# Seven products for eight in u and v, and the S5 projection placed after v, in a hybrid decoder block

## The chip, the cores and the metric

The kernel runs on one core of one Trainium2 chip. The metric is the time of one execution on the device in microseconds, the median of three runs. The engines are TensorE (PE: matrix products into banks of PSUM; weights are loaded by PEld beside it), VectorE (DVE), ScalarE (ACT), GpSimd (POOL) and SyncE (SP), which here only issues transfers. Each engine works through its own list of instructions in order: an instruction that waits holds up all that stands behind it on that engine, and nothing else.

## The reference

One layer for 1024 tokens of 1024 channels in float32. Only the first sub-layer is touched; cross-attention and the SwiGLU FFN follow it unchanged.

```python
h = rms_norm(x, g_mix_pre)
z = h @ w_in                        # columns: u 1024 | v 1024 | S5 512 | gate A 1024 | gate B 1024
u, v = split(gelu(z_gm))
v = layer_norm(v, ln_g, ln_b)       # over the 1024 channels of a token
sv = einsum('gts,bnsgc->bntgc', tril(w_s), v) + b_s   # 8 groups of 128 channels, chunks of 128 tokens
y_gm = u * sv
y = gelu(s5_scan(z_s5))             # 32 groups of 16 channels, 64 complex states each
y_s5 = y * sigmoid(y @ w_glu)
merged = sigmoid(z_ga) * (y_gm @ w_br_gm) + sigmoid(z_gb) * (y_s5 @ w_br_s5)
x = x + rms_norm(merged @ w_mix_out, g_mix_post)
```

## The kernel before

A float32 product is made of three products in the format fp32r: each operand is split into a high half and the rest, and `mm3` adds hi·hi, hi·lo and lo·hi. One matmul takes 128 channels and gives 128 by 512 results, so that a block of `n` steps over the contracted channels costs 3n matmuls. To split a tile is a cast on ACT (`put`, L525, for data; `split`, L102, for weights) and a subtraction on DVE (L526, L103), which reads what the cast wrote.

All engines follow an order that the program writes out by hand. The main line is the products; between groups of them `sub()` lets each background generator (`bg`) take a step, and where a step lands there its instructions stand in every engine's list. Weights come as a stream: `make_plan` lists them in the order of use, `load` (SP queue, three raw buffers `wr`) and `split` work up to three ahead. Tiles of data are 38 slots `act` of 128 by 1024; PSUM has 8 banks `ps`.

The stages of the first sub-layer (`go`, L1559): keys and values of the memory with x's norm beside them; `s5_in`; `gates` (both gates to DRAM, with the S5 scan, `s5_gen`, beside them); then

- `s5_out` (L805): the first two blocks of u, then `drain()`, which runs the background to its end: GELU of the four tiles of the scan's output y (L744), 32 transposes of it (L754), and their splits. Then y @ w_glu with its sigmoid, and the product with w_br_s5 (`bs`), scaled by gate B, to DRAM;
- `v_phase` (L859): v, tokens on the partitions, two halves of 512 columns, each for two halves of the tokens in four banks each. GELU reads the bank and sums along the row (L899). After the second column half `ln` runs beside what follows: four squares with sums (L873), a reciprocal root in some dozen tiny operations, and per tile of 128 tokens one operation on 128x1024 (scale by `ln_g`) and eight on 128x128 (`ln_b`, written by groups, `vg`);
- `gm_phase` (L920): u's blocks 2 to 7; beside blocks 4 to 7 the gates, 8 groups of two halves: four products of 128x128 with the turned triangle, bias, times u, split;
- `merge` (L956): both branches to `merged`.

Line numbers below are of before; the changed kernel has the same helpers some lines later (L515 is L519 there, L133 L134, L136 L140, L102 and L103 L103 and L104, L525 and L526 L529 and L530).

Of the kernel before, what the change touches and what calls it, by code (L numbers as in the profile page):

```python
# [36 lines left out]
class Builder:  # L37
    def __init__(self, ctx, tc, ins):
# [13 lines left out]
        self.live = 0  # L52
        self.raws, self.pairs = {}, {}

# [11 lines left out]
    def sub(self):  # L66
        """called between groups of products"""
# [15 lines left out]
    def pump(self, n=1):  # L83
        while n and self.nsp < len(self.plan) and self.live < NWS - 1 and self.nsp < self.cur + LOOK:
            self.split()
            n -= 1

    def load(self):
        while self.nd < len(self.plan) and self.nd < self.nsp + NRAW:
# [34 lines left out]
    def rsqrt_ops(self, y, v, t):  # L124
        """y = 1 / sqrt(v): a first guess from the bits, three steps of Newton"""
# [6 lines left out]
    def tt(self, out, a, b, op):  # L132
        self.nc.vector.tensor_tensor(out=out, in0=a, in1=b, op=op)  # L133

# [13 lines left out]
    def vexp(self, o, x, k, r, i):  # L148
        """o = exp(x); k, r: room; i: int32 room"""
# [58 lines left out]
    def s5_params_a(self):  # L208
# [25 lines left out]
        # powers of a = mag (cs, sn), pq: P | Q for d = 0..8  # L234
# [19 lines left out]
        # co = (a - 1) / lam  # L254
# [20 lines left out]
        # mag^8  # L275
# [14 lines left out]
    def s5_params_b(self):  # L290
        """tables of e^{i 8 theta c}: 16 entries low, 8 entries high; and a^{7-k}"""
# [45 lines left out]
    def s5_params_c(self):  # L337
        """b and c with the states on the partitions"""
# [49 lines left out]
    def s5_a(self, b):  # L388
        """a^{7-k} B and C a^d"""
# [26 lines left out]
    def s5_b(self, b):  # L416
        """U, the B side turned, and what a chunk's tokens give within it"""
# [34 lines left out]
    def s5_c(self, b):  # L452
        """the phases, the chunks' parts, the scan over chunks"""
# [40 lines left out]
    def s5_d(self, b):  # L494
        """the chunks' outputs"""
# [21 lines left out]
    def mm3(self, ps, a, b, first, last, more=False):  # L517
        """float32's product: a = hi + lo, b = hi + lo, each part exact in float32r"""
# [4 lines left out]
    def put(self, dst, src):  # L523
        """dst = (hi, lo) of what lies in src"""
# [10 lines left out]
    def tblock(self, ps, w, c, xs, n=8, every=2):  # L535
        """ps[128 columns of w, tokens]"""
# [5 lines left out]
    def nblock(self, pss, w, k0, xs, last):  # L542
        """pss[t][tokens, 512 columns of w]"""
# [34 lines left out]
    def turn(self, xs, gi, dst, ks=range(8)):  # L578
        """transposes of four row tiles, scaled by the gain, split"""
# [1043 lines left out]
```

## Time and profile before

| | before |
|---|---|
| median of three runs | 1670.44 us (1669.47, 1670.44, 1670.87) |
| span of the profiled execution | 1668.2 us |
| the profiled execution's own time | not recorded apart from its span; the median lies 2.2 us above the span |
| PE busy | 1639.3 us, 98% |
| DVE, ACT, POOL busy | 1130.1, 637.3, 5.9 us |
| u0 and u1's end, drain, `glu`, `bs` | 366.19 to 445.50 us |
| v's products | 445.50 to 532.54 us |
| u2 to u7 with the gates | 532.54 to about 620 us |

A row of the timeline gives the start, the duration and the work, with a count where equal instructions are merged; the bracket tells how long the engine had been idle and whom it waited for. The page's chain follows the work that ended last back from the end: the engine that holds most of it sets the time. A window gives the busy time of every engine in a stretch, and the clock that TensorE was granted there (1.00 is its higher level of 2.4 GHz).

### The profile page before, as it was taken

To read this page: it belongs to the slowest core of one execution; us is meant where nothing else is said; L and a number is where in the kernel's file an instruction comes from. 1 tells how busy PE (TensorE), PEld (TensorE's weight loads), DVE (VectorE), ACT (ScalarE), POOL (GpSimd) and SP (SyncE) were. 2 spreads that over 40 slices of the span, in tenths; PEclk is the share of its full clock that TensorE was granted. 3 is DMA by queue.
4 is the path that set the end of the run, shared out by engine and by line. 5 is a ranking of instruction groups with operands and counts; after the bars stand their busy time and mean duration, and the time that the engine had idled before them with its cause. 6 is when DMAs were issued, how large, how long until landed. Compare 5 with 4: busy or idle time off the path is not lost.

```text
span 1668.2 us, 20774 instructions
## 1 busy us (share of the span) xinstructions
PE 1639.3 (98%) x7856; PEld 1374.1 (82%) x7856; DVE 1130.1 (68%) x2049; ACT 637.3 (38%) x1104; POOL 5.9 (0%) x13
## 2 busy tenths in 40 slices
PE   6999999999999999999999999999999999999998
PEld 6898878887888888888888888888888888888886
DVE  5679779867214665447854577686778777666778
ACT  6632212234124232235553447753233223244454
POOL 0000000000000000000000000000000000000000
PEclk9999999999999999999999999999999999999999
DMA  8622222213511225434523153674544446363634
GB/s 278 196 59 92 68 71 93 88 50 113 203 51 54 60 81 171 151 140 146 170 76 115 63 186 117 207 243 131 187 141 165 157 153 206 129 237 130 218 112 171
DMA packets 198772, 228.58 MB, mean 137 GB/s; under 512 B 13296, under 2 KB 137232, under 8 KB 198672
## 3 DMA queue, kind: packets, MB, share of 16 engines
q1 hardware_dynamic: 173328, 171.27, 31.9%
q10 hardware_dynamic: 24768, 53.88, 8.7%
q0 software_dynamic: 576, 2.10, 0.3%
q8 instruction: 62, 1.02, 0.2%
q14 instruction: 38, 0.31, 0.1%
HBM read 169.15 MB, written 56.36 MB: 135 GB/s over the span
## 4 chain that ended last, share of the span: by engine, by line
PE 89%; DVE 6%; ACT 2%; issue 1%; DMA 1%; ACTq 1%; SPq 0%; DVEq 0%
PE ps L515 85%; DVE act L133 2%; PE ps L583 1%; DVE ws L103 1%; DVE act L526 1%; ACTq L449 1%; ACT jk L571 0%; PE ps L1132 0%; ACT ws L102 0%; PE ps L1086 0%; DVE act L136 0%; ACT act L525 0%; PE ps L504 0%; DVE act L140 0%; PE ps L474 0%
## 5 line engine op out<-in xcount | busy, mean ns | idle before, releaser
L515 PE MATMUL ps<-act,ws 128*128 128x512 f32 (+1 forms) x4248 | 973.3, 387 | 3.8 <-DVE act L526 2.5
L515 PEld LDWEIGHTS ps<-act,ws 128*128 128x128 f32 x4248 | 780.4, 188 | 162.3 <-DVE act L526 4.7
L515 PE MATMUL ps<-ws,act 128*128 128x512 f32 x1440 | 342.8, 395 | 0.0
L515 PEld LDWEIGHTS ps<-ws,act 128*128 128x128 f32 x1440 | 279.4, 207 | 46.9
L133 DVE TENSOR_TENSOR act<-act 128x512 f32<-128x512 f32 (+6 forms) x513 | 281.8, 578 | 7.1 <-ACT act L1418 0.5
L103 DVE TENSOR_TENSOR ws<-wr,ws 128x1024 fp32r<-128x1024 f32 x114 | 139.2, 1222 | 126.9 <-ACT ws L102 124.6
L515 PE MATMUL ps<-ws 128*128 128x512 f32 x852 | 193.3, 389 | 0.0
L515 PEld LDWEIGHTS ps<-ws 128*128 128x128 f32 x852 | 159.9, 188 | 33.2
L133 DVE TENSOR_TENSOR act<-ps,act 128x512 f32<-128x512 f32 x178 | 120.9, 684 | 60.5 <-PE ps L515 55.6
L102 ACT CAST ws<-wr 128x1024 fp32r<-128x1024 f32 x114 | 119.5, 1048 | 104.9 <-PE ps L515 69.5
L1211 ACT CAST ws<-tm 128x512 fp32r<-128x512 f32 x88 | 54.8, 622 | 168.3 <-PE ps L515 113.3
L133 DVE TENSOR_TENSOR ws<-act,ws 128x512 fp32r<-128x512 f32 x93 | 64.2, 690 | 67.4 <-ACT ws L1418 51.8
L133 DVE TENSOR_TENSOR ws<-tm,ws 128x512 fp32r<-128x512 f32 x88 | 60.8, 691 | 59.5 <-ACT ws L1211 58.5
L525 ACT CAST act<-act 128x512 fp32r<-128x512 f32 (+1 forms) x72 | 46.1, 643 | 114.4 <-DVE act L133 114.0
L133 DVE TENSOR_TENSOR ws<-wr,ws 128x512 fp32r<-128x512 f32 x115 | 78.7, 685 | 15.2 <-ACT ws L1211 15.2
L515 PE MATMUL ps<-act 128*128 128x256 f32 (+2 forms) x488 | 83.3, 318 | 0.0
L526 DVE TENSOR_TENSOR act<-act 128x512 fp32r<-128x512 f32 (+1 forms) x72 | 51.8, 720 | 42.5 <-ACT act L525 42.5
L515 PEld LDWEIGHTS ps<-act 128*128 128x128 f32 x488 | 72.3, 189 | 8.3
L1418 ACT CAST ws<-act 128x512 fp32r<-128x512 f32 x71 | 44.2, 622 | 89.5 <-PE ps L515 48.3
L526 DVE TENSOR_TENSOR act<-ps,act 128x512 fp32r<-128x512 f32 x56 | 40.8, 748 | 47.7 <-ACT act L525 47.7
L136 DVE SCALAR_TENSOR_TENSOR act<-act,st 128x128 f32<-128x128 f32 (+2 forms) x100 | 58.7, 639 | 0.6
L525 ACT CAST act<-ps 128x512 fp32r<-128x512 f32 x56 | 35.6, 668 | 45.3 <-PE ps L515 38.0
(133 smaller groups left out, 902.4 us busy)
## 6 DMA issues: line engine op xcount, KB each, us to landing
wr<-in_ffn_w_gu_dram SPq DMA_DIRECT2D x39, 512.0 KB, 4.6
actd<-act ACTq DMA_DIRECT2D x77, 256.0 KB, 2.1
wr<-actd SPq DMA_DIRECT2D x38, 512.0 KB, 3.7
wr<-in_w_in_dram SPq DMA_DIRECT2D x36, 512.0 KB, 3.6
act<-in_ffn_w_gu_dram SPq DMA_DIRECT2D x22, 512.0 KB, 4.8
act<-in_ffn_w_down_dram SPq DMA_DIRECT2D x44, 256.0 KB, 4.4
pd<-act ACTq DMA_DIRECT2D x17, 512.0 KB, 4.2
act<-pd SPq DMA_DIRECT2D x34, 256.0 KB, 3.6
```

Of the source, the lines that this page charges most:

```text
L102: self.nc.scalar.copy(hi, t)
L103: self.nc.vector.tensor_tensor(out=lo, in0=t, in1=hi.bitcast(F), op=ALU.subtract)
L133: self.nc.vector.tensor_tensor(out=out, in0=a, in1=b, op=op)
L136: self.nc.vector.scalar_tensor_tensor(out=out, in0=a, scalar=s, in1=b, op0=op0, op1=op1)
L449: nc.scalar.dma_start(tv[16 * k:16 * k + 16, :, 16 * k:128], kv[:, :, 0:128 - 16 * k])
L515: self.nc.tensor.matmul(ps, a, b, start=start, stop=stop, skip_group_check=more)
L525: self.nc.scalar.copy(dst[0], src)
L526: self.nc.vector.tensor_tensor(out=dst[1], in0=src, in1=dst[0].bitcast(F), op=ALU.subtract)
L583: self.nc.tensor.transpose(ps[:, t * 128:t * 128 + 128], x[:, k * 128:k * 128 + 128], self.ident)
L1211: self.nc.scalar.copy(t[:, 0:512], now)
L1418: nc.scalar.copy(w[:, h[0]], src)
```

## The change

Blocks 2 to 7 of u are taken in pairs (2,3), (4,5), (6,7): the products of two blocks by two halves of the contracted channels and two halves of the tokens, which are eight products of halves, become seven by Winograd's form of Strassen's scheme. v is taken in the same form, by halves of channels, columns and tokens, in eight banks: X and Y, four each. The seven are named 11, 21, T1, T2, 22, T3, T4 after the side of h that they take. The sums of h (`h_sums`: 24 operations) are formed on GpSimd during the S5 scan, spilled to DRAM and taken back and split (`h_split`) when the scan is over; the sums of weights (`uv_sides`: 28 operations on 128x512) are formed on GpSimd one product ahead, and split (`w_ops`). What a product gives beside its bank is added on DVE from PSUM.

The order becomes u0, u1, u's pairs, v, then `s5_out` with the gates (`gm_gen`) beside it. u is spilled to DRAM and taken back by the gates. The scan's output y is spilled after its GELU; `y_turn` takes it back and transposes it beside v's last product. `ln` uses two operations on 128x1024 per tile, and loads `ln_g` and `ln_b` itself; `ln(1)` (the second half of the tokens) starts beside v's product 21, `ln(0)` after T4.

```diff
     def go(self, out):
...
         self.gates()
+        self.bg(self.w_ops(self.uv_sides()), 1)
+        for m in range(2):
+            self.u_block(m)
+        self.plain = True
+        self.u_pairs()
+        self.v_phase()
         self.s5_out()
-        self.v_phase()
-        self.gm_phase()
         self.merge()
...
+    def h_sums(self):
...
+        for k in range(4):
+            a, b = self.slot(), self.slot()
+            for t, kk in ((a, k), (b, k + 4)):
+                hi, lo = self.hT[kk]
+                self.gt(t, hi.bitcast(F), lo.bitcast(F), A)
+                yield 2
+            (a0, a1), (b0, b1) = ((t[:, 0:512], t[:, 512:1024]) for t in (a, b))
+            self.gt(a0, a1, a0, S)
+            self.gt(a1, b1, a1, S)
+            nc.gpsimd.dma_start(self.td[2 * k], a)
...
+            self.gt(b1, b1, a0, S)
+            self.gt(b0, b0, b1, S)
+            nc.gpsimd.dma_start(self.td[2 * k + 1], b)
...
         for q in range(4):
-            y = self.yq.pop(q)
-            self.yT.append(self.pair())
-            for jh in range(2):
+            self.nc.scalar.dma_start(self.yd[q], self.yq.pop(q))
+        y = None
+        yield from self.h_split()
...
     def s5_out(self):
         nc = self.nc
-        for m in range(2):
-            self.u_block(m)
-        self.drain()
+        while len(self.yT) < 4 or not self.yok:
+            self.sub()
...
+    def y_turn(self):
+        ys = []
+        for q in range(4):
+            ys.append(self.slot())
+            self.nc.sync.dma_start(ys[q], self.yd[q])
+        yield 2
+        for q in range(4):
+            self.yT.append(self.pair())
+            for jh in range(2):
+                ps = self.bank()
+                for j in range(4):
+                    o = (4 * jh + j) * 128
+                    self.nc.tensor.transpose(ps[:, j * 128:j * 128 + 128], ys[q][:, o:o + 128], self.ident)
...
+                self.put(dst, ps.rearrange("p (j c) -> p j c", j=4))
+                yield 1
...
-            self.rms(st, 4)
-            if not vg:
-                vg.extend(self.slot() for _ in range(8))
+            yield from self.rms_slow(st, 4)
+            if half:
+                self.lng = self.bcast(i["gm_ln_g"][0]), self.bcast(i["gm_ln_b"][0])
+            lg, lb = self.lng
             for t in range(4):
-                yield 2
+                yield 1
                 v = vt[4 * half + t]
                 self.stt(v, v, st[:, 40 + t:41 + t], lg, ALU.add, ALU.mult)
-                for g in range(8):
-                    o = slice(g * 128, g * 128 + 128)
-                    n = 4 * half + t
-                    self.stt(vg[g][:, n * 128:n * 128 + 128], v[:, o], st[:, 16 + t:17 + t], lb[:, o], ALU.mult, ALU.add)
+                self.stt(v, v, st[:, 16 + t:17 + t], lb, ALU.mult, ALU.add)
...
+        run(X, "T3", False)
+        del self.fxs["T3"]
+        for t in range(4):
+            v = vt[4 + t]
+            self.tt(v[:, h1], X[t], v[:, h1], ALU.add)
+            gelu(v[:, h1], v[:, h1], st(1, 1, t))
+        v = None
+        self.bg(ln(1))
+        run(Y, "21", True)
...
+        for t in range(4):
+            self.tt(vt[t][:, h0], Y[t], vt[t][:, h0], ALU.add)
+            gelu(vt[t][:, h0], vt[t][:, h0], st(0, 0, t))
+        Y = None
+        self.bg(self.y_turn(), 1)
+        run(X, "T4", False)
...
+        for t in range(4):
+            gelu(vt[t][:, h1], X[t], st(0, 1, t))
+        X = None
+        self.bg(ln(0))
```

On PE, before, from the end of the scan: the last 18 products of u1 (L515), the 32 transposes of y (L754), `glu` and `bs` (288), and v (384).

```order
L515 MATMUL ps<-act,ws 128x512 x18
L754 MATMUL ps<-ident,act 128x128 x32
L515 MATMUL ps<-act,ws 128x512 x288
L515 MATMUL ps<-ws,act 128x512 x384
```

On PE, after, the same stretch: u1's rest and u's pairs (270), v up to the middle of T4 (306), then the transposes of y (L1071) between T4's products, `glu`, the triangles (L1176) and the first gate's four 128x128 products.

```order
L519 MATMUL ps<-act,ws 128x512 x270
L519 MATMUL ps<-ws,act 128x512 x306
L1071 MATMUL ps<-ident,act 128x128 x4
L519 MATMUL ps<-ws,act 128x512 x6
L1071 MATMUL ps<-ident,act 128x128 x4
L519 MATMUL ps<-ws,act 128x512 x6
L1071 MATMUL ps<-ident,act 128x128 x4
```

On PE, after, from T4's last six products on: the last three transposed groups, `glu`'s first 36 products, the triangles and the first gate.

```order
L519 MATMUL ps<-ws,act 128x512 x6
L1071 MATMUL ps<-ident,act 128x128 x12
L519 MATMUL ps<-act,ws 128x512 x36
L1176 MATMUL ps<-ident,act 128x128 x4
L519 MATMUL ps<-act,ws 128x512 x6
L1176 MATMUL ps<-ident,act 128x128 x4
L519 MATMUL ps<-act,ws 128x512 x6
L519 MATMUL ps<-act 128x128 x4
```

The transposes stood as one block ahead of `glu`; now they stand in T4, which still holds four banks, and the gates stand in `glu` and `bs`, the first 48 products after the last transposes.

On DVE, after, from the statistics of `ln(1)` to the subtractions of y's splits: L104 splits weights, L140 on 128x1024 is `ln`, L134 `act<-ps,act` empties product 21's banks, L530 splits y.

```order
L104 TENSOR_TENSOR ws<-wr,ws 128x1024
L140 SCALAR_TENSOR_TENSOR st<-st 128x4 x2
L134 TENSOR_TENSOR st<-st 128x4
L140 SCALAR_TENSOR_TENSOR st<-st 128x4 x2
L134 TENSOR_TENSOR st<-st 128x4
L140 SCALAR_TENSOR_TENSOR st<-st 128x4
L140 SCALAR_TENSOR_TENSOR act<-act,st 128x1024 x2
L134 TENSOR_TENSOR act<-ps,act 128x512 x4
L140 SCALAR_TENSOR_TENSOR act<-act,st 128x1024 x2
L104 TENSOR_TENSOR ws<-wr,ws 128x1024
L140 SCALAR_TENSOR_TENSOR act<-act,st 128x1024 x4
L530 TENSOR_TENSOR act<-ps,act 128x4x128 x3
L104 TENSOR_TENSOR ws<-wr,ws 128x1024
L530 TENSOR_TENSOR act<-ps,act 128x4x128 x4
```

Before, the eight subtractions of y (L526) had only weights' splits beside them, and `ln` stood behind v; now eight `ln` operations, four emptyings and two weights' splits stand in one row ahead of y's first subtraction.

On DVE, after, from the end of the statistics of `ln(0)` to the second pair of its four tiles: L134 with `tm` and L530 `act<-act` are `glu`'s product with the sigmoid and its split, L140 on 128x1024 is `ln(0)`, which the first gate's products read.

```order
L140 SCALAR_TENSOR_TENSOR st<-st 128x4 x2
L134 TENSOR_TENSOR st<-st 128x4
L140 SCALAR_TENSOR_TENSOR st<-st 128x4
L134 TENSOR_TENSOR tm<-act 128x512
L134 TENSOR_TENSOR act<-act,tm 128x512
L530 TENSOR_TENSOR act<-act 128x512
L140 SCALAR_TENSOR_TENSOR act<-act,st 128x1024 x4
L134 TENSOR_TENSOR tm<-act 128x512
L134 TENSOR_TENSOR act<-act,tm 128x512
L530 TENSOR_TENSOR act<-act 128x512
L140 SCALAR_TENSOR_TENSOR act<-act,st 128x1024 x4
```

Before, `ln`'s operations had u's blocks 2 and 3 beside them; now all eight of `ln(0)` and three groups of `glu` come ahead of the first gate's last product.

On SP, after, from the last weights of v (L924): `glu`'s and `bs`'s weights (L94), then `ln_g` and `ln_b`, then y (L1063).

```order
L924 DMA act<-in_w_in_dram 128x1024 x5
L94 DMA wr<-in_s_w_glu_dram 128x4x256 x2
L94 DMA wr<-in_w_br_s_dram 128x4x256 x2
L579 DMA act<-in_gm_ln_g_dram 128x1024
L579 DMA act<-in_gm_ln_b_dram 128x1024
L1063 DMA act<-yd 128x1024 x4
L94 DMA wr<-in_w_br_s_dram 128x4x256 x2
```

On SP, before, `ln_g` and `ln_b` (L575) stood ahead of v's last weights:

```order
L835 DMA act<-gbd 128x1024 x2
L93 DMA wr<-in_w_in_dram 128x2x512
L575 DMA act<-in_gm_ln_g_dram 128x1024
L575 DMA act<-in_gm_ln_b_dram 128x1024
L93 DMA wr<-in_w_in_dram 128x2x512 x2
L93 DMA wr<-in_w_in_dram 128x8x128 x6
```

They now stand behind a load into the raw buffer that the first of `glu`'s weights has to leave, and ahead of y.

## Rows read from the trace of the kernel before

**Rows 1.** The page: busy time of TensorE, and the last chain by engine.

```profile
PE 1639.3 (98%) x7856; PEld 1374.1 (82%) x7856; DVE 1130.1 (68%) x2049; ACT 637.3 (38%) x1104; POOL 5.9 (0%) x13
...
PE 89%; DVE 6%; ACT 2%; issue 1%; DMA 1%; ACTq 1%; SPq 0%; DVEq 0%
```

**Rows 2.** Timeline, PE, 366 to 446 us: start, duration, work [idle before, releaser].

```profile
366.19 4.34 PE L515 MATMUL ps<-act,ws 128*128 128x512 f32 x18
370.38 3.65 PE L754 MATMUL ps<-ident,act 128*128 128x128 f32 x32
373.79 0.48 PE L515 MATMUL ps<-act,ws 128*128 128x512 f32 x1
...
380.85 64.81 PE L515 MATMUL ps<-act,ws 128*128 128x512 f32 x278 [0.36 <-DVE act L526]
```

**Rows 3.** Windows: busy per engine (instructions), TensorE's granted clock, DMA share, GB/s.

```profile
80.00:120.00 40.00, 40.00 (x209) 38.88 (x210) 30.15 (x160) 10.40 (x27) 0.00 (x0) 1.00 0.25 65
120.00:180.00 60.00, 60.00 (x286) 50.22 (x286) 55.12 (x174) 16.47 (x34) 0.00 (x0) 1.00 0.28 91
370.00:385.00 15.00, 12.69 (x57) 9.03 (x56) 11.66 (x13) 12.41 (x14) 0.00 (x0) 0.77 0.11 36
```

**Rows 4.** Timeline, PE, 440 to 540 us: v's products.

```profile
445.50 87.20 PE L515 MATMUL ps<-ws,act 128*128 128x512 f32 x384
```

**Rows 5.** Timeline, PE, 614 to 622 us: the last gate before the merge.

```profile
618.70 0.50 PE L515 MATMUL ps<-act,ws 128*128 128x512 f32 x1 [0.54 <-ACT act L525]
```

**Rows 6.** Timeline, POOL, whole span: its select on the triangles.

```profile
543.29 1.09 POOL L906 TENSOR_SCALAR_AFFINE_SELECT act<-act 128x1024 f32<-128x1024 f32 x1 [470.25 <-DVE st L142]
```

**Rows 7.** Timeline, DVE, 508 to 548 us: small operations beside it.

```profile
543.41 0.99 DVE L133 TENSOR_TENSOR st<-st 128x4 f32<-128x4 f32 x1
```

**Rows 8.** Lines by form, ACT, 366 to 620 us: count | busy, mean ns | idle before.

```profile
L744 ACT ACTIVATE act<-act 128x1024 f32<-128x1024 f32 x4 | 3.9, 1052 | 0.0
L525 ACT CAST act<-act 128x512 fp32r<-128x512 f32 x23 | 14.3, 620 | 47.0 <-DVE act L133 47.0
L525 ACT CAST act<-ps 128x512 fp32r<-128x512 f32 x8 | 7.9, 1154 | 0.2 <-PE ps L754 0.2
L899 ACT ACTIVATE act<-ps 128x512 f32<-128x512 f32 x16 | 9.6, 599 | 39.4 <-PE ps L515 39.4
L873 ACT ACTIVATE jk<-act,st 128x1024 bf16<-128x1024 f32 x8 | 9.2, 1149 | 4.1 <-DVE st L140 4.0
L873 ACT ACTIVATION_READ_ACCUMULATOR jk<-act,st 128x1 f32 x8 | 1.5, 187 | 0.0
L102 ACT CAST ws<-wr 128x1024 fp32r<-128x1024 f32 x20 | 21.0, 1050 | 57.9 <-PE ps L515 36.9 <-DVE act L133 11.1 <-DMA mbd<-act 9.9
L821 ACT ACT_TABLE_LOAD x1 | 1.3, 1283 | 0.0
```

**Rows 9.** Timeline, ACT, 402 to 446 us: the issue of one transfer.

```profile
409.40 0.36 ACTq L852 DMA_DIRECT2D mbd<-act  x1
```

**Rows 10.** Lines by form, DVE, 366 to 700 us.

```profile
L103 DVE TENSOR_TENSOR ws<-wr,ws 128x1024 fp32r<-128x1024 f32 x28 | 34.3, 1224 | 45.8 <-ACT ws L102 45.8
L526 DVE TENSOR_TENSOR act<-act 128x512 fp32r<-128x512 f32 x39 | 27.0, 692 | 26.9 <-ACT act L525 26.9
L133 DVE TENSOR_TENSOR act<-ps,act 128x512 f32<-128x512 f32 x31 | 21.3, 691 | 46.5 <-PE ps L515 46.5
L136 DVE SCALAR_TENSOR_TENSOR act<-act,st 128x1024 f32<-128x1024 f32 x8 | 10.2, 1278 | 0.0
L526 DVE TENSOR_TENSOR act<-ps,act 128x512 fp32r<-128x512 f32 x8 | 8.4, 1116 | 8.0 <-ACT act L525 8.0
L136 DVE SCALAR_TENSOR_TENSOR st<-st 128x4 f32<-128x4 f32 x12 | 2.0, 163 | 0.4
```

**Rows 11.** DMA issues: size, median us from issue to landing.

```profile
act<-gbd SPq DMA_DIRECT2D x8, 512.0 KB, 6.0
act<-in_gm_ln_g_dram SPq DMA_DIRECT2D x1, 512.0 KB, 6.1
```

More of the change, by code (lines that the diff above doesn't have):

```diff
@@ L694, in xgen @@
             self.bg(self.s5_gen(), 5)
+            self.bg(self.h_sums(), 2)
         self.bg(xgen())
@@ L758, in s5_in, with hx @@
+    def hx(self, name, k):
+        while name not in self.sides:
+            self.sub()
+        if name in ("11", "T1", "21", "22"):
+            o = 0 if name in ("11", "21") else 512
+            return tuple(x[:, o:o + 512] for x in self.hT[k + (4 if name[0] == "2" else 0)])
+        return self.fx(name, k)
     def s5_in(self):
@@ L803, in u_block, with later, w_ops @@
                 self.rel()
+        self.later(self.ud[m], u)
+    def later(self, *new):
+        while self.late:
+            self.nc.scalar.dma_start(*self.late.pop(0))
+        if new:
+            self.late.append(new)
+    def w_ops(self, gen):
+        while self.nsp < self.bar:
+            yield 1
+        now = None
+        while True:
+            t = None
+            if now is not None:
+                while self.live >= NWS:
+                    yield 1
+                t = self.ws.tile([P, 1024], R, name="ws", tag="ws")
+                self.live += 1
+                self.nc.scalar.copy(t[:, 0:512], now)
+            nxt = next(gen, ())
+            if nxt:
+                for x in nxt[1]:
+                    self.gt(*x)
+            if t is not None:
+                self.tt(t[:, 512:1024], now, t[:, 0:512].bitcast(F), ALU.subtract)
+                self.ops.append(t)
+            if nxt == ():
+                self.bar = len(self.plan)
+                return
+            now = nxt[0]
+            yield 1
@@ new lines, in ln, with run @@
+            if not half:
+                lg = lb = self.lng = None
+                self.vok = True
+        X, Y = ([self.bank() for _ in range(4)] for _ in range(2))
+        def run(ps, name, first):
+            for k in range(4):
+                x = self.hx(name, k)
+                w = self.take()
+                for t in range(4):
+                    c = slice(t * 128, t * 128 + 128)
+                    self.mm3(ps[t], tuple(z[:, c] for z in x), (w[:, h0], w[:, h1]), first and k == 0, k == 3, not first)
+                    if t % 2:
+                        self.sub()
+                self.live -= 1
+                x = w = None
@@ new lines, in v_phase @@
+        st = lambda half, cb, t: sums[half][:, 32 + cb * 4 + t:33 + cb * 4 + t]
+        gelu = lambda o, x, acc: nc.scalar.activation(out=o, in_=x, func=AF.Gelu_apprx_tanh, accum_out=acc)
+        run(X, "11", True)
+        for t in range(4):
+            vt[t] = self.slot()
+            nc.scalar.copy(vt[t][:, h0], X[t])
+        run(Y, "T1", True)
+        for k in range(4):
+            self.hT[k] = None
+        for t in range(4):
+            vt[4 + t] = self.slot()
+            nc.scalar.copy(vt[4 + t][:, h1], Y[t])
```

245 lines of the change are left out of this document (189 added, 56 removed).

## The prediction

> **What bounds the kernel now.** I read the page first, then PE's timeline over the stages that the change touches, then windows over the S5 scan, then the groups by line of ACT and DVE, for durations. PE is busy for 98% of the span and carries 89% of the chain that ended last [rows 1]: the kernel is bound by TensorE's products, so products that go away are worth their time, and anything that keeps PE waiting is paid in full. Between the scan's end at 366.19 and the merge, PE waits in two places only. One is y's turn: its 32 transposes start at 370.38, the products that need y's splits begin at 373.79, and ten of them last until 380.85 [rows 2], 7.06 us in place of 2.27 at the 0.227 us per product that v shows (87.20 us for 384 [rows 4]). In that window the granted clock is 0.77 [rows 3], a mean over stretches at 1.2 and 2.4 GHz. The other is the last gate, 0.54 us [rows 5].
>
> **What goes.** Each pair of u's blocks takes 84 products for 96, three times: 36 fewer. v takes 336 for 384: 48 fewer. 84 x 0.227 = 19.1 us. The stall at y's turn, 7.06 - 2.27 = 4.8 us, and the slower products behind it, 64.81 us for 278 where 63.0 are due [rows 2], 1.8 us: 6.6 in all. The last gate's 0.5: the gates now end inside `bs`. Sum of gains: **26.2 us**. They are gains only if what replaces those stalls is hidden.
>
> **What comes, beside the S5 scan.** `h_sums` are 8 operations of 128x1024 and 16 of 128x512 on GpSimd. The trace has no such sum; the nearest row is the select on 128x1024, 1.09 us [rows 6], which gives 8 x 1.09 + 16 x 0.55 = 17.5 us. For the upper end I double it, 35 us, since a sum reads two tiles and the select one. The same moment shows what such work does to DVE: a tiny operation on two inputs that starts 0.12 us behind the select takes 0.99 us [rows 7], where the tiny ones of its kind take 0.16 [rows 10], and ends with the select. So I take DVE's operations on two tiles to be held while GpSimd works. DVE is idle for 40.00 - 30.15 = 9.9 us between 80 and 120 and for 60.00 - 55.12 = 4.9 us between 120 and 180 [rows 3], and that is the stretch on which the scan's first results depend. What does not fit into 14.8 idle us delays the scan and then PE, which has only products in a fixed order to cover it: 17.5 - 14.8 = 2.7 us by the row, 35 - 14.8 = 20 us by its double; below it nothing, if idle time takes all of it; a gain is excluded, since no instruction leaves this stretch. I take 3 us, by the nearest row.
>
> The Trainium skill (GPSIMD Engine Reference, section 3.1) gives 4497 ns for a float32 `tensor_tensor` of 2048 elements per partition on GpSimd, and calls elementwise work DVE's. By it, as an estimate, the 24 sums are 36 us and the term 21 instead of 3. It also names (SBUF — State Buffer, "SBUF: two separate sides") the shared port pair as a lock held for a whole instruction, which would be the cause of the 0.99; the rule holds both ways, so that GpSimd's sums would wait for DVE as well. The trace agrees with the holding at that one place and shows no sum's price.
>
> **What comes, in u's pairs (T1).** The splits of the sums start when the scan is over. From 366.2 ACT has to do, in this order: a copy and a GELU of a bank and another copy (0.6 each [rows 8]), four GELUs 3.9, five issues of transfers at 0.36 [rows 9], six casts of 0.62 ahead of the first cast for T1, and that one: about 12.0 us, so it is there at 378.2. PE has 18 products of u1 and 24 of the first two halves ahead, 42 x 0.227 = 9.5, and stands at 375.7. T1's last quarter needs seven more casts and a subtraction of 0.69 [rows 10], 383.2, where PE would use it 9 products in, at 377.8. **5.4 us** lost. The taking back of sums is covered by this only as long as a transfer of 512 KB lands in some 6 us [rows 11].
>
> **What comes, from v's T3 to the first gate.** I count from t = 0, the end of T3's products. PE's own path: 66 products (21, and 18 of T4) to the first transposes of y at 15.0; the fifth group of transposes at 22.2; the end of T4 and of all 32 transposes (3.65 [rows 2]) at 25.4; the last quarter of `glu`'s first block at 27.5; the first gate's last product at 37.7 (48 products and 12 small ones further).
>
> - Statistics. Emptying a bank 0.69, GELU with its sum 0.60 + 0.19, a weights' cast and subtraction 0.62 + 0.69, two tiny operations 0.33: 3.1. Four squares at 1.15 + 0.19: 8.5. Behind them on ACT stands the cast of `glu`'s first weights, 1.05, and on DVE its subtraction, 1.22: 10.8 [rows 8, 10].
> - The loads. SP holds a load of `bs`'s weights that needs the raw buffer which this subtraction frees, and behind it `ln_g`, `ln_b` and the four of y. `ln_g` lands 6.1 us after its issue [rows 11]: 16.9. y, at 6.0, lands little later.
> - First transposes. They need a bank; all eight belong to X and Y, and Y's are emptied on DVE behind two operations of `ln(1)`, 2 x 1.28, and one emptying: 20.2. PE stands at 15.0: 5.2 us lost.
> - Fifth group. It needs the bank of the first, which y's first subtraction frees. Ahead of that on DVE: three emptyings 2.1, six operations of `ln(1)` 7.7, a split 1.22, and itself 1.12: 32.3. PE would be there at 22.2 + 5.2 = 27.4: 4.9 more.
> - `glu`. Seven more of y's subtractions 7.8, a split 1.22, two tiny ones; on ACT T4's four GELUs 3.2, one square 1.34 and y's casts of 1.15 stand between: about 45.5. PE's own path has 27.5, so the loss is now 18.0 in all.
> - First gate. It needs all four tiles of `ln(0)`. ACT: three squares 4.0, a cast 1.05 (a table load 1.28 and the sigmoid lie beside DVE): 49.5. DVE: a split 1.22, twelve tiny ones 2.0, eight operations of `ln(0)` 10.2, and three of `glu`'s groups that stand between them, each three operations of 0.69 and a cast of 0.62 that DVE waits for, 8.1: **71.0**. PE's path has 37.7: **33.3 us** lost so far.
> - Start of `bs`. It needs the last quarter of `glu`. DVE has 24 operations of 0.69 and a split ahead, 17.8, and waits in eight of its splits for a cast, 5.0: 22.8. PE has 57 products and four gates' small ones, 14.8: **8.0** more.
>
> What hid `ln` before were u's blocks 2 and 3 and, for the loads, v's own products; both now come ahead of it. Behind this the gates and `bs` give DVE less per group than PE, so that nothing more is late. The sums for v and u on GpSimd (28 of 128x512) lie beside stretches in which DVE has room; I cost them at nothing, at most at the 0.55 us each that DVE is held, which PE then does not see outside T1.
>
> **Clock.** After a wait PE ran slower: 1.8 us behind the stall in [rows 2]. I take it twice, behind T1 and behind `bs`'s start: 3.6. It could be none, or five times as many waits' worth, 9.
>
> **Sum.** 3 + 5.4 + 33.3 + 8.0 + 3.6 = 53.3 us of losses against 26.2 of gains: + 27.1. The profiled span is 1668.2, and the median 1670.44 lies 2.2 above it; 1668.2 + 27.1 + 2.2 = 1697.5, **1698 us**. With the GpSimd term from 0 to 8, the clock from 0 to 9 and a fifth off or on the two DVE chains (8 us), the forecast's own range is 1685 to 1711.
>
> **Rivals.**
> - *GpSimd is the heavier cost.* If a sum costs twice the select, 20 us stand where I put 3: 1715. For it: two inputs for one, and DVE at 92% of 120 to 180. Against it: the sums start at about 72, ahead of the window, and may run where DVE waits for other things.
> - *The row on DVE is shorter than counted: half the waits.* If `ln_g` lands earlier (by 3) and the operations around it overlap so that the last two terms come to 20 instead of 41.3: 1677. For it: some of `glu`'s work may fit into DVE's waits. Against it: every term is a duration of a row, and DVE does them in order.
> - *Hidden after all (the other side).* The place is T4's first transposes: were the loads of `ln_g` and y not held by SP, and `ln(1)` done before T4, then y's splits and `ln(0)` would start 20 us earlier and lie beside T4 and `glu`. Nothing is then paid there: 1670.4 - 26.2 + 12.0 = 1656. It decides at waits of 14 us from T3 to `bs` in place of 41.3: below it the change is faster. For it speaks that PE has 25 us of products there; against it, that DVE's and ACT's work from T3 to the gate alone is 71.
> - *No difference*, the waits and the gains equal: 1670.
>
> **How the numbers follow.** Forecast 0.66; heavier GpSimd 0.14; half the waits 0.08; hidden 0.08; equal 0.04. A measurement of this kernel tells 0.2%, 3.3 us, from no change. Faster than 1667.1: 0.08 and a little of the others, 0.09. Within: 0.04. Slower: 0.87. The range 1673 to 1721 leaves out hidden and equal, 0.12, and the far end of the heavier GpSimd, some 0.06.
>
> **What would show it.** In the profile after: a PE wait of some 5 us ahead of T4's first transposes (released by DVE or by the transfer of y), further ones at the fifth group, in `glu`, and the longest, some 15 us, at the first gate's 128x128 products, released by `ln`; one more at the start of `bs`; about 5 us at T1; 84 products fewer; the granted clock below 1.00 behind them. SP shows `ln_g` issued behind the wait for the raw buffer. In the scan PE waits for DVE by a few us more than now. I am wrong if PE stays 98% busy from v's T3 to `bs`, or if GpSimd's sums take far more or less than 1.1 us per 1024.

## The result, and the profile after

The changed kernel takes 1722.57 us (median; 1720.71 to 1723.82), beside 1670.21 us for the kernel before on the same chip (1669.47 to 1670.87): ratio 1.0309, 95% interval 1.0294 to 1.0323. It is slower, as forecast, but by 52.4 us where 27.1 were worked out, and 1.6 us beyond the range's upper end. The profiled execution's span is 1719.7 us.

The page of after, to be read against [rows 1]: the 84 products are gone (7856 to 7772), PE's busy share is down from 98 to 95%, and its share of the last chain from 89 to 61%. GpSimd has 94.5 us of work for 5.9.

```profile
PE 1640.7 (95%) x7772; PEld 1370.4 (80%) x7772; DVE 1199.2 (70%) x2065; ACT 669.7 (39%) x1172; POOL 94.5 (5%) x73
...
PE 61%; DVE 2%; ACT 1%; issue 0%; DVEq 0%; ACTq 0%
```

PE's timeline of after tells where the time went (start, duration, work, in brackets the wait and its releaser). Shown are rows that follow waits, and those that serve as marks below; shorter waits are left out.

```profile
132.16 31.34 PE L519 MATMUL ps<-act,ws 128*128 128x512 f32 x130 [4.39 <-DVE ws L104]
175.53 1.09 PE L433 MATMUL ps<-ident,act 128*128 128x128 f32 x4 [8.84 <-DVE act L134]
...
387.36 0.49 PE L507 MATMUL ps<-act 128*128 128x128 f32 x2 [3.21 <-DVE act L134]
389.28 0.79 PE L508 MATMUL ps<-act 128*128 128x128 f32 x2 [1.43 <-DVE act L134]
...
393.57 11.74 PE L519 MATMUL ps<-act,ws 128*128 128x512 f32 x46
...
461.34 3.04 PE L519 MATMUL ps<-act,ws 128*128 128x512 f32 x12 [2.74 <-DVE act L134]
464.21 69.52 PE L519 MATMUL ps<-ws,act 128*128 128x512 f32 x306
539.58 1.11 PE L1071 MATMUL ps<-ident,act 128*128 128x128 f32 x4 [5.85 <-DVE act L134]
...
551.03 0.66 PE L1071 MATMUL ps<-ident,act 128*128 128x128 f32 x4 [1.21 <-DVE act L530]
...
562.82 7.65 PE L519 MATMUL ps<-act,ws 128*128 128x512 f32 x26 [0.64 <-DVE act L530]
...
587.78 0.80 PE L519 MATMUL ps<-act 128*128 128x128 f32 x2 [1.72 <-DVE act L140]
...
611.48 1.95 PE L519 MATMUL ps<-act,ws 128*128 128x512 f32 x3 [4.10 <-ACT act L529]
...
752.88 47.31 PE L519 MATMUL ps<-ws,act 128*128 128x512 f32 x208
```

Three marks divide the loss. The scan ends (the first u product behind its last group) at 393.57, before at 366.19 [rows 2]: **27.4 us late**. The product with `w_mix_out` (L519, `ps<-ws,act`) starts at 752.88. In before it starts here, in the same view:

```profile
701.61 18.75 PE L515 MATMUL ps<-ws,act 128*128 128x512 f32 x82
```

That is 51.3 late, so from the scan's end to the merge **23.9** more are lost; the rest of the kernel loses next to nothing (the spans differ by 51.5). v itself runs without a wait up to T4's first transposes, 306 products in 69.52, the 0.227 each of [rows 4]. The gates cost no wait at the merge any more [rows 5].

The scan's stretch in windows, to be read against [rows 3], with the same columns: between 80 and 120 DVE gets 54 operations done for 160 and GpSimd is busy for 33.43; in 120 to 180 PE has 46.77 busy of 60 at a granted clock of 0.89, where it had 60 at 1.00.

```profile
80.00:120.00 40.00, 38.88 (x200) 37.04 (x201) 34.28 (x54) 9.35 (x26) 33.43 (x26) 0.96 0.41 131
120.00:180.00 60.00, 46.77 (x197) 38.75 (x197) 56.20 (x247) 14.30 (x30) 0.00 (x0) 0.89 0.22 70
```

The groups by line and form on GpSimd over the whole span of after give what the trace of before did not have, a sum's price (count | busy, mean ns | idle before):

```profile
L137 POOL TENSOR_TENSOR act<-act 128x512 f32<-128x512 f32 x18 | 25.8, 1434 | 0.8
L137 POOL TENSOR_TENSOR act<-act 128x1024 f32<-128x1024 f32 x8 | 19.9, 2500 | 62.2 <-DVE act L140 62.1
```

A sum of 128x1024 takes 2.50 us in the mean, 2.3 times the select [rows 6], a half 1.43. And DVE's timeline of after shows what it does to the scan's tables:

```profile
89.73 10.20 DVE L140 SCALAR_TENSOR_TENSOR act<-act 128x32 f32<-128x32 f32 x6
...
102.15 7.75 DVE L146 TENSOR_SCALAR act<-act 128x32 int32<-128x32 f32 x1
```

The same six operations in DVE's timeline of before:

```profile
82.75 1.33 DVE L136 SCALAR_TENSOR_TENSOR act<-act 128x32 f32<-128x32 f32 x6
```

Six operations that took 1.33 us take 10.20, and a single one, with one input, takes 7.75. Most of the 10.20 is the second of the six (DVE's timeline, 90 to 96 us):

```profile
89.96 6.42 DVE L140 SCALAR_TENSOR_TENSOR act<-act 128x32 f32<-128x32 f32 x1
```

GpSimd's timeline of after at these places, in narrow windows (equal lines stand as one row, here two sums of 128x1024 and one half; the single row is the second half):

```profile
90.32 6.00 POOL L137 TENSOR_TENSOR act<-act 128x1024 f32<-128x1024 f32 x3
...
96.39 1.29 POOL L137 TENSOR_TENSOR act<-act 128x512 f32<-128x512 f32 x1
...
103.89 5.96 POOL L137 TENSOR_TENSOR act<-act 128x1024 f32<-128x1024 f32 x3
...
109.93 1.34 POOL L137 TENSOR_TENSOR act<-act 128x512 f32<-128x512 f32 x1
```

The two long operations of DVE end at 96.38 and 109.90: just behind three sums that GpSimd runs without a gap (they end at 96.32 and 109.85), and before the next, ahead of which GpSimd stands idle for 0.08 us (in the program the second half overwrites what the first one reads). From 82 to 115 us eleven operations of 128x32 on DVE take over 1 us, 26.9 together, and each ends 0.04 to 0.06 us after a GpSimd operation behind which GpSimd pauses or issues a transfer. DVE shows as busy while it waits for GpSimd.

### The profile page after: what moved, and what is told of

It is laid out like the page before. It is cut to its first block, busy times and chain, and to the rows that moved or that the text cites. A ratio compares the mean times of both kernels' runs of the same rounds, so it can differ in the third digit from the quotient of the medians.

```text
span 1719.7 us, 20904 instructions
## 1 busy us (share of the span) xinstructions
PE 1640.7 (95%) x7772; PEld 1370.4 (80%) x7772; DVE 1199.2 (70%) x2065; ACT 669.7 (39%) x1172; POOL 94.5 (5%) x73
## 4 chain that ended last, share of the span: by engine, by line
PE 61%; DVE 2%; ACT 1%; issue 0%; DVEq 0%; ACTq 0%
PE ps L519 60%; PE ps L1392 0%; PE ps L1346 0%; PE ps L587 0%; DVE act L134 0%; DVE ws L104 0%; DVE act L140 0%; ACT jk L575 0%; DVE act L530 0%; ACT act L1334 0%; DVE st L140 0%; ACT ws L103 0%; DVE st L1330 0%; ACT act L529 0%; ACT act L1267 0%
## 5 line engine op out<-in xcount | busy, mean ns | idle before, releaser
L519 PE MATMUL ps<-act,ws 128*128 128x512 f32 (+1 forms) x4212 | 975.0, 390 | 18.8 <-ACT act L529 7.5
L519 PEld LDWEIGHTS ps<-act,ws 128*128 128x128 f32 x4212 | 778.6, 190 | 179.2 <-ACT act L529 8.4
L519 PE MATMUL ps<-ws,act 128*128 128x512 f32 x1392 | 336.5, 398 | 0.0
L519 PEld LDWEIGHTS ps<-ws,act 128*128 128x128 f32 x1392 | 271.9, 208 | 45.8
L134 DVE TENSOR_TENSOR act<-act 128x512 f32<-128x512 f32 (+6 forms) x513 | 286.3, 587 | 7.1 <-ACT act L1678 0.5
L519 PE MATMUL ps<-ws 128*128 128x512 f32 x852 | 193.3, 389 | 0.0
L519 PEld LDWEIGHTS ps<-ws 128*128 128x128 f32 x852 | 159.9, 188 | 33.2
L104 DVE TENSOR_TENSOR ws<-wr,ws 128x1024 fp32r<-128x1024 f32 x100 | 124.5, 1247 | 78.8 <-ACT ws L103 78.6
L134 DVE TENSOR_TENSOR act<-ps,act 128x512 f32<-128x512 f32 x199 | 134.7, 685 | 45.0 <-PE ps L519 42.1
L134 DVE TENSOR_TENSOR ws<-act,ws 128x512 fp32r<-128x512 f32 x107 | 74.0, 691 | 90.4 <-ACT ws L1678 51.8
L134 DVE TENSOR_TENSOR ws<-tm,ws 128x512 fp32r<-128x512 f32 x108 | 78.1, 725 | 84.1 <-ACT ws L1471 58.7
L103 ACT CAST ws<-wr 128x1024 fp32r<-128x1024 f32 x100 | 104.8, 1048 | 63.9 <-PE ps L519 33.8
L134 DVE TENSOR_TENSOR ws<-wr,ws 128x512 fp32r<-128x512 f32 x130 | 91.1, 701 | 38.5 <-ACT ws L881 23.4
L529 ACT CAST act<-act 128x512 fp32r<-128x512 f32 (+1 forms) x88 | 55.3, 639 | 136.7 <-DVE act L134 135.8
L530 DVE TENSOR_TENSOR act<-act 128x512 fp32r<-128x512 f32 (+1 forms) x88 | 65.5, 751 | 51.0 <-ACT act L529 50.8
L519 PE MATMUL ps<-act 128*128 128x256 f32 (+2 forms) x488 | 86.8, 324 | 11.3 <-DVE act L140 11.3
L519 PEld LDWEIGHTS ps<-act 128*128 128x128 f32 x488 | 74.6, 194 | 21.2 <-DVE act L140 8.8
L530 DVE TENSOR_TENSOR act<-ps,act 128x512 fp32r<-128x512 f32 x56 | 41.2, 751 | 42.6 <-ACT act L529 42.6
L529 ACT CAST act<-ps 128x512 fp32r<-128x512 f32 x56 | 36.9, 667 | 49.2 <-PE ps L519 38.0
```

The source lines that it names most:

```text
L103: self.nc.scalar.copy(hi, t)
L104: self.nc.vector.tensor_tensor(out=lo, in0=t, in1=hi.bitcast(F), op=ALU.subtract)
L519: self.nc.tensor.matmul(ps, a, b, start=start, stop=stop, skip_group_check=more)
L529: self.nc.scalar.copy(dst[0], src)
L530: self.nc.vector.tensor_tensor(out=dst[1], in0=src, in1=dst[0].bitcast(F), op=ALU.subtract)
```

## The experiments

The kernel before took between 1669.4 and 1670.3 us beside them. Each is an edit of after unless it says otherwise.

### h's sums on DVE

```diff
 def h_sums(self):        # all six lines
-    self.gt(...)
+    self.tt(...)
```

> The changed kernel with the 24 sums of h on VectorE in place of GpSimd, at the same steps, nothing else moved. Theory (while GpSimd forms sums it holds VectorE's tiny operations, each for a sum or more): these operations take 0.2 us again, VectorE gets 8 x 1.22 + 16 x 0.69 = 20.8 us of work of its own with some 15 idle us to take it, so that the scan ends some 6 us late through the sums in place of 20, and the six early sums of weights still cost their 7: the scan ends near 380 us in place of 393.6, the time near 1709 us (1703 to 1714). Rival (slots, the spills or the order of the steps delay the scan, not the engine): the scan still ends near 393, 1719 to 1726 us. Rival (it is only the amount of work that VectorE cannot hide): 1722 or more.

1712.41 us, ratio 1.0256 (1.0239 to 1.0273). DVE by form, 70 to 180 us:

```profile
L140 DVE SCALAR_TENSOR_TENSOR act<-act 128x32 f32<-128x32 f32 x36 | 6.9, 192 | 1.2
```

In after the same 36 take 19.5 us, 541 ns in the mean. The scan ends 11 us earlier than in after (PE's timeline), with one wait left for its turned tables:

```profile
163.61 1.09 PE L433 MATMUL ps<-ident,act 128*128 128x128 f32 x4 [7.01 <-DVE act L134]
...
382.47 10.73 PE L519 MATMUL ps<-act,ws 128*128 128x512 f32 x43
```

So the hold by GpSimd is real. But DVE's own sums (1216 ns each of 128x1024) seem to cost something too: how much is shown by the kernel without sums, further on.

### The weights' sums on DVE

```diff
 def w_ops(self, ...):
-    self.gt(*x)
+    self.tt(*x)
```

> The changed kernel with the 28 sums of weights on VectorE in place of GpSimd, the sums of h still on GpSimd. Theory: the wait of 3.2 and 1.4 us and the slower clock at the scan's last group come from six of these sums holding VectorE; with 6 x 0.69 us of its own work in their place the last group ends 4 to 6 us earlier, the rest is hidden beside u's and v's products, 1717 us (1714 to 1720). Rival (GpSimd is free there and VectorE is the engine that has no room): 1722 to 1730 us.

1718.45 us, 1.0292 (1.0277 to 1.0308). The scan's end moved by less than a microsecond (392.9), and the waits of its last group are still 2.72 and 1.43; what was gained, 4.1 us in all, came mostly behind it, in u's pairs. So for that group it isn't decisive on which engine the weights' sums run.

### The weights' operations later

```diff
-        self.bg(self.w_ops(self.uv_sides()), 1)
+        self.bg(self.w_ops(self.uv_sides()), 12)
```

> The changed kernel with the first weights' splits and sums 11 steps later, behind the scan's last group instead of ahead of it. Theory (four splits and three sums ahead of the scan's last group make it late by 3.2 and 1.4 us and let the clock fall): those waits go and the scan ends some 6 us earlier, of which the first products of u's pairs give some back, since their sides are then split beside the taking back of h's sums: 1717 to 1721 us. Rival (the last group is late for the earlier delay alone): the scan still ends near 393, 1722 or more.

1721.92 us, 1.0309 (1.0294 to 1.0325). PE's timeline:

```profile
384.15 0.49 PE L508 MATMUL ps<-act 128*128 128x128 f32 x2 [0.22 <-DVE act L134]
...
386.40 9.81 PE L519 MATMUL ps<-act,ws 128*128 128x512 f32 x42
399.76 0.79 PE L519 MATMUL ps<-act,ws 128*128 128x512 f32 x1 [3.55 <-ACT act L529]
```

The scan ends 7.2 us earlier: those 7 us of after were the weights' first operations, which stand ahead of the scan's last group. Nothing is kept, since the splits are then late for T1, where 3.55 us and more are waited. It is the same work, paid on either side of the mark.

### Everything on DVE, h's sums spread into the scan's groups

```diff
-            self.bg(self.h_sums(), 2)
+            self.bg(self.h_sums(), 40)
 ...                      # in h_sums gt -> tt, in w_ops gt -> tt
-                yield 2
+                yield 4
```

> The changed kernel with all sums (of h and of weights) on VectorE, and the sums of h spread over the scan's groups, one every four steps from the 40th on. Theory (what delays the scan is GpSimd's hold on VectorE's tiny operations while the scan's tables are made; in the groups VectorE is idle some 4 us in 27): the tables are ready in time again, TensorE's 4.4 and 8.8 us of waits are gone, the scan ends near 375 us in place of 393.6, and the time is 1700 us (1695 to 1706). Rival (VectorE's idle time in the groups cannot be used, 20.8 us of sums delay the scan wherever they stand): 1708 to 1714 us.

1713.47 us, 1.0264 (1.0247 to 1.0281), where 1700 was expected: a miss. The tables wait for nothing any more, but the groups behind them do (PE's timeline):

```profile
221.05 0.80 PE L507 MATMUL ps<-act 128*128 128x128 f32 x2 [5.15 <-DVE act L134]
...
386.51 10.33 PE L519 MATMUL ps<-act,ws 128*128 128x512 f32 x43
```

The rival's number was right: the gaps that DVE shows between the groups took up only a part of the sums. In before DVE is idle for 23.6 us between 200 and 360; for 15.9 of them it waits, at the head of its row, for ACT's casts of weights (L103 for L102), for 5.4 for PE. What is put there comes late in the next group.

### h's sums on GpSimd, spread

The delays of the experiment above, with the sums left on GpSimd.

> The changed kernel with the sums of h still on GpSimd, but one every four steps from the 40th on, beside the scan's groups, where VectorE's operations last 0.7 us and not 0.2. Theory (a sum holds VectorE for what is left of it, whatever the length of VectorE's operation, so what counts is GpSimd's 41 us less VectorE's idle time there): the tables are ready in time, the groups late instead; the scan ends near 390 to 400 us and the time is 1719 to 1730 us. Rival (only tiny operations suffer, since each waits for a whole sum): the scan ends near 376 and the time is 1705 us.

1725.11 us, 1.0332 (1.0318 to 1.0347): no better than after. DVE's timeline beside a run of sums, and PE's:

```profile
201.47 4.81 DVE L134 TENSOR_TENSOR act<-act 128x512 f32<-128x512 f32 x4
```

```profile
224.02 0.80 PE L507 MATMUL ps<-act 128*128 128x128 f32 x2 [5.30 <-DVE act L134]
...
394.41 10.54 PE L519 MATMUL ps<-act,ws 128*128 128x512 f32 x43
```

Four operations of 128x512 take 4.81 us, where 0.69 each is 2.8: the longer ones are held too, and spreading the sums did not bring the scan's end forward. The second group waits 5.30 us here and 5.15 with the sums on DVE.

### h's sums left out

```diff
-                self.gt(t, hi.bitcast(F), lo.bitcast(F), A)
+                nc.scalar.copy(t, hi.bitcast(F))
 ...
-            self.gt(a0, a1, a0, S)        # and the three others of halves
```

> The kernel after with h's sums left out: each of the eight tiles is filled by a copy on ACT (about 1 us of 128x1024) and spilled and taken back as before, the sixteen operations of halves are gone, so T1 to T4 take other data. Nothing of h's sums is left on GpSimd or on DVE. Theory (the sums themselves are what makes the scan late, by holding DVE's operations; the weights' splits ahead of the scan's last group are the rest): DVE's operations of 128x32 are back at about 0.2 us and those into int32 at 0.18, the turned tables at 130 and 175 wait for nothing, the scan's last group still waits as in w_late's counterpart, so that the scan ends at 373 to 377 in place of 393.6, and the whole at 1702 to 1707 us, ratio 1.019 to 1.022. Rival (the room that the sums take, their spills and the tiles they hold delay the scan): the scan ends at 388 or later, 1716 us or more.

1704.71 us, 1.0205 (1.0191 to 1.0219), as the theory had it. The windows, and PE's timeline:

```profile
80.00:120.00 40.00, 40.00 (x208) 38.88 (x209) 30.06 (x160) 14.20 (x31) 4.00 (x6) 1.00 0.43 136
120.00:180.00 60.00, 60.00 (x286) 50.21 (x285) 55.15 (x174) 16.47 (x34) 0.00 (x0) 1.00 0.29 96
```

```profile
157.57 0.60 PE L433 MATMUL ps<-ident,act 128*128 128x128 f32 x4
...
367.83 0.49 PE L507 MATMUL ps<-act 128*128 128x128 f32 x2 [3.21 <-DVE act L134]
...
374.04 1.20 PE L519 MATMUL ps<-act,ws 128*128 128x512 f32 x2
```

In both windows PE and DVE are as in before again, although spills, slots and loads are as in after. The scan ends at 374.04: of its 27.4 us the sums are 19.5, and in the 7.9 left stand the waits of the last group, which the later weights' operations took away.

### ln's loads earlier

```diff
-            if half:
-                self.lng = self.bcast(i["gm_ln_g"][0]), self.bcast(i["gm_ln_b"][0])
...
         v = None
+        self.lng = self.bcast(i["gm_ln_g"][0]), self.bcast(i["gm_ln_b"][0])
         self.bg(ln(1))
```

> The changed kernel with the loads of ln_g and ln_b issued ahead of v's product 21 in place of behind the statistics. Theory (a chain on VectorE, started by the landing of ln_g, sets each later wait): VectorE's 5.3 us of waiting for ln_g go, the first transposes still wait for y's own landing, 3 to 4 us in place of 5.9, all later waits move up: 1718 us (1716 to 1720). Rival (TensorE's waits there have other causes, a bank or ScalarE): 1721 to 1724 us.

1717.97 us, 1.0292 (1.0276 to 1.0307). PE's timeline:

```profile
535.15 0.63 PE L1071 MATMUL ps<-ident,act 128*128 128x128 f32 x4 [0.65 <-DMA act<-yd]
...
581.96 0.80 PE L519 MATMUL ps<-act 128*128 128x128 f32 x2 [4.49 <-DVE act L140]
```

The first transposes wait 0.65 in place of 5.85, and the gate's products still wait for `ln`: the wait for the load is gone, DVE's row of operations behind it is not. 4.6 us of the time are saved.

### The gates later

```diff
-        self.bg(self.gm_gen(), 10)
+        self.bg(self.gm_gen(), 22)
...
-                yield 2
+                yield 1 + half
```

> The changed kernel with the first gate 12 steps later (behind two blocks of the second projection's start instead of in the middle of the first) and the gates closer together. Theory (between v's third product and the merge VectorE's row is the bound, 71 us of it ahead of the first gate): the 11 us of waits at the first gate go, but the start of the second projection waits some 12 us longer for the same row, and the denser gates wait again behind it: 1715 to 1727 us. Rival (the gates merely stand too early): 1709 us, 13 us less, with no new wait.

1717.94 us, 1.029 (1.0275 to 1.0306), 4.6 us less than after where the rival had 13. The first gates wait for nothing; the start of `bs` does, 6.66 and 3.60, and further on three products among the gates, 0.6 to 1.1:

```profile
595.54 1.95 PE L519 MATMUL ps<-act,ws 128*128 128x512 f32 x3 [6.66 <-ACT act L529]
601.09 4.50 PE L519 MATMUL ps<-act,ws 128*128 128x512 f32 x9 [3.60 <-ACT act L529]
```

It is the work of DVE and ACT that is late, whatever of PE's stands first behind it.

### Less work behind v

`ln_g` and `ln_b` taken into the gates as factors per channel, the normalisation one operation on ACT per tile, y loaded before product 21, the gates later:

```diff
-                self.stt(v, v, st[:, 40 + t:41 + t], lg, ALU.add, ALU.mult)
-                self.stt(v, v, st[:, 16 + t:17 + t], lb, ALU.mult, ALU.add)
+                nc.scalar.activation(out=v, in_=v, func=AF.Identity, scale=st[:, 16 + t:17 + t], bias=st[:, 44 + t:45 + t])
```

> The changed kernel with VectorE relieved between v's T3 and the merge: y's four loads issued ahead of product 21; ln's scale and shift by ln_g and ln_b folded into the gates (ln_g as a per-channel factor where the bias is added, ln_b times the triangle's row sums in the bias), the normalisation itself as one ScalarE operation per tile, so that 16 operations of 1.28 us leave VectorE; ln of the second half behind y's splits; the gates 8 steps later and closer. Theory (the waits from T4 to the second projection are VectorE's row of 71 us): the first transposes wait at most 1 us, the first gates not at all, in the two projections 5 to 10 us remain: 1695 us (1690 to 1702). Rival (ScalarE or the loads take VectorE's place): 1705 us or more. The scan is as in the changed kernel.

1705.41 us, 1.0212 (1.0197 to 1.0227): 17 us less than after, where 27 were expected. T4's transposes no longer wait; a new wait stands at the products that form the row sums:

```profile
587.15 2.04 PE L519 MATMUL ps<-act 128*128 128x512 f32 x2 [12.41 <-DVE act L1194]
```

L1194 fills a tile with ones, in 0.17 us, and is queued on DVE behind `glu`.

### Both together

This and "everything on DVE".

> The edits of the kernel with all sums on VectorE and of the one with VectorE relieved behind v, together. If the two losses are separate stretches, they add: some 22 and 27 us off 1722, 1673 us (1666 to 1681), about level with the kernel before (1670). Rival (one hides the other): 1685 us or more.

1696.97 us, 1.0167 (1.015 to 1.0184). The two add up (9.1 and 17.2 us apart, 25.6 together), but each is smaller than thought, and with both the kernel is still slower than before.

### Both, with the new wait removed

The ones at the program's start, the normalisations behind `glu`, the gates one step apart.

> The kernel of both edits (sums on VectorE, VectorE relieved behind v) with the tile of ones for the row sums made at the start, ScalarE's normalisations behind the first projection, and the gates one step apart from then on. Theory (its last wait of 12.2 us, for a tile that VectorE writes behind the first projection's chain, and the chain of casts and subtractions between ScalarE and VectorE are what is left there): that wait shrinks to some 4 us, the gates wait a few us in all: 1688 us (1683 to 1693). Rival (the sum of VectorE's work behind v is still the bound): 1695 us or more.

1698.03 us, 1.017 (1.0155 to 1.0186): nothing gained. The one wait of 12 us is now eight of 0.2 to 1.8, 7.9 us together (one row of PE's timeline, then the window over them):

```profile
580.83 0.63 PE L519 MATMUL ps<-act 128*128 128x128 f32 x2 [1.77 <-ACT act L1103]
```

```profile
540.00:600.00 60.00, 49.35 (x208) 38.58 (x209) 35.27 (x65) 31.38 (x43) 0.00 (x0) 0.86 0.32 113
```

PE is busy for 49.35 of these 60 us, at a clock of 0.86. The rival's number was right, its reason is not shown: DVE is busy for 35.27 of the 60 and ACT for 31.38, so neither one's own work fills the stretch. PE waits for ACT's casts (L529) and normalisations (L1103), which alternate with DVE's operations; that this chain between the two sets the time is likely, and no run took it apart.

### The kernel before, with three blocks of u ahead of y

The stall at y's turn is the one gain of the change that needs none of the rest. In before:

```diff
 def s5_out(self):         # and the plan of the weights alike
-        for m in range(2):
+        for m in range(3):
             self.u_block(m)
 ...
-        for m in range(2, 8):
+        for m in range(3, 8):
```

> The kernel before (eight products each, old order) with u's third block ahead of the S5 projection in place of behind v: y's transposes and splits then stand between that block's products, and ln and the gates keep five blocks as their cover. Theory (the change's gain at y's turn, 6.6 us, was there without the rest of it: it takes products of u beside the turn and nothing else): the ten slow products and the slower clock behind them go, 1664 us (1662.5 to 1666). Rival (the splits of y are late beside a block too, or ln loses its cover): 1668 to 1672 us.

1663.44 us (1662.96 to 1664.15), ratio 0.9961 (0.9948 to 0.9973): faster than both kernels. The 32 transposes now stand between u2's products, without a wait, and the clock, 0.77 in [rows 3], is 1.00 in the window from 366 to 400 (PE's timeline, then the window):

```profile
369.32 0.60 PE L754 MATMUL ps<-ident,act 128*128 128x128 f32 x4
369.68 1.64 PE L515 MATMUL ps<-act,ws 128*128 128x512 f32 x6
```

```profile
366.00:400.00 34.00, 34.00 (x167) 28.19 (x166) 21.36 (x24) 24.03 (x29) 0.00 (x0) 1.00 0.10 32
```

## Why the prediction was right in one half and wrong in the other

**Wrong: the term beside the S5 scan.** It stood as 3 us, bounded at 0 and 20; the scan ended 27.4 us late. Two steps of it failed.

- The price of a sum and what it holds (3 us; measured 19.5, with the sums left out against after). The select [rows 6] was the nearest row and the wrong one to take: the 24 sums are 8 x 2.50 + 16 x 1.43 = 42.9 us by their means and not 17.5, more than the double that bounded it. The prediction's own sign of being wrong, far more than 1.1 us per 1024, was there. And the step "What does not fit into 14.8 idle us delays the scan" is not what happens. The eleven held operations from 82 to 115 take 26.9 us, where 0.2 each would be 2.2; they stand in the one row of short operations that makes the scan's tables, and DVE's idle time at other places does not take up what this row loses. Of the 24.7 us, 19.5 reach the scan's end. Spreading the sums on GpSimd did not help, and doing them on DVE (8 x 1.22 + 16 x 0.69 = 20.8 us) still cost 8.4 us of the scan (382.5 for 374.0) ahead of its groups and 12.5 (386.5, with the weights' sums on DVE too) among them. That 19.5 lies inside the old bound of 20 is luck, from two errors of opposite sign: the work was more than twice as much, and 23.4 us of it, not 14.8, did not show at the scan's end.
- The weights' operations "beside stretches in which DVE has room; I cost them at nothing" (measured 7.2 to 7.9). The first splits and sums stand ahead of the scan's last group on DVE. Taken away from there they are paid at T1, 1721.92 for 1722.57: they find no room on DVE and ACT around the scan's end, and the T1 term was counted from a scan that ended without them.

The rival "GpSimd is the heavier cost" named the first with 20 us, and its 1715 is what the sums alone come to (1698 + 16.5); with the weights' 7.9 it is 1722.

The Trainium skill (GPSIMD Engine Reference, section 3.1) had the better price: from its 4497 ns per 2048 elements the estimate was 36 us of sums and a term of 21; the trace has 42.9 and 19.5. That the 21 comes so close is luck of the same kind, since it too takes off 14.8 idle us.

**Right: the terms from the scan's end to the merge.** They were 5.4 + 33.3 + 8.0 + 3.6 - 26.2 = 24.1 us; 23.9 were measured. The single terms are off by up to some 2 us, so the agreement to 0.2 is partly luck. By steps, with t = 0 at the end of T3's products (240 of the 306 in the row at 464.21: 518.7):

| step | predicted | after |
|---|---|---|
| first transposes | t = 20.2 | 539.58, t = 20.9 |
| fifth group | 32.3 | 551.03, 32.3 |
| last quarter of `glu`'s first block | 45.5 | 562.82, 44.1 |
| first gate's last product | 71.0 | 587.78, 69.1 |
| lost to the first gate | 33.3 | 69.1 - 37.7 = 31.4 |
| gate to the start of `bs` | 22.8 | 611.48 - 587.78 = 23.7 |
| T1, with half of the clock's 3.6 | 7.2 | 464.21 - 393.57 - 270 x 0.227 = 9.3 |

T1's 9.3 hold 2.74 that no term named: the wait at 461.34, where the last pair's T4 needs the bank that DVE has yet to empty of T3.

The other causes are the ones named. The loads of `ln_g` and y stand on SP behind the one that waits for the raw buffer, which goes out as soon as DVE's split has freed it (DVE's timeline, then SP's: issue, its length):

```profile
528.34 1.23 DVE L104 TENSOR_TENSOR ws<-wr,ws 128x1024 fp32r<-128x1024 f32 x1 [0.17 <-ACT ws L103]
...
529.60 0.37 SPq L94 DMA_DIRECT2D wr<-in_w_br_s_dram  x1
530.06 0.46 SPq L579 DMA_DIRECT2D act<-in_gm_ln_g_dram  x1
...
531.08 2.49 SPq L1063 DMA_DIRECT2D act<-yd  x4
```

and DVE stands still for it:

```profile
536.12 1.28 DVE L140 SCALAR_TENSOR_TENSOR act<-act,st 128x1024 f32<-128x1024 f32 x1 [5.28 <-DMA act<-in_gm_ln_g_dram]
```

One half of "hidden after all" was tried: with the load early, 4.6 us come back, not 20; the row of DVE behind it is too long, as the argument against that rival had it. With most of that row gone as well (less work behind v) it is 17.2. The shape of the waits was wrong: where one of some 15 us was named at the first gate, there are four of 1.7 to 4.5, 11.3 together.

**The gains are as counted.** 84 products are gone. That y's turn was worth its 6.6 us shows in the kernel before with three blocks of u ahead of it: 6.8.

**What stays open.** Whether v and u in seven products can pay at all here. With h's sums taken away altogether 34.8 us are still missing to before, and the shorter work behind v gives 17.2 back; the two were not run together. If they added, as the two edits of "both together" nearly did, some 17.6 us would still be missing, by this estimate. Open too is why the two longest of DVE's held operations were held across the seams between GpSimd's operations, where the next begins as the last one ends.

## What to carry to other kernels

Where the trace has no row for an operation on another engine, a row with fewer inputs is not its price: here the sum took 2.3 times the select. Take a wide bound, and measure it first. Ask which row of operations the new work may hold. Idle time averaged over a window hides nothing if others wait for a row of short operations that is held. A stall is often to be had alone: three blocks of u in place of two ahead of the transposes gave 6.8 us with none of the other costs.

## What was not expected of the hardware

GpSimd's back-to-back operations hold DVE for longer than one of them: an operation of 0.18 us took 7.75, while GpSimd ran two fills and three sums without a gap. The Trainium skill (SBUF — State Buffer, "SBUF: two separate sides") has a lock that lasts for one instruction of whichever engine came first. From that one would take DVE to be held for one operation of GpSimd at a time; the rows at 89.96 and 102.15 show it held through several in a row, up to GpSimd's next pause.

It is no fixed order. With the sums spread, an operation of 128x512 that starts at 236.65 got its turn at such a seam: it took 2.88, and the GpSimd half behind the seam 1.74 in place of 1.29. So GpSimd waits for DVE too.

Operations with one input were held as well as those with two: the one of 7.75 has one, and those at 99.96 and 111.79 took 1.30 and 1.73 for 0.18.
